# An MLP's down projection on one Trainium2 core: sums of weight blocks in a buffer of their own, conversions by the pair, and a fourth sweep

## The chip, the core and the metric

The kernel runs on one core of a Trainium2 chip. Its engines run side by side, each through its own list of instructions in order, and wait for each other by semaphores: TensorE (PE in the profile; PEld is its weight load), VectorE (DVE), ScalarE (ACT), GpSimd (POOL, unused here) and SyncE (SP, whose queue issues the loads). The metric is the device time of one execution in microseconds (us). Before the change its median over three runs is 2785.03 us (2783.8 to 2786.33).

## The reference

A decoder trunk with two layers, 256 tokens, a width of 2048 and float32 throughout:

```
h = h + retention(rms_norm(h))                 # layer 0
h = h + mlp(rms_norm(h)); h = h + gated_embedding(h, p)
k, v = rms_norm(h) @ w_kv
h = h + block_sparse_attention(rms_norm(h), k, v)   # layer 1
h = h + mlp(rms_norm(h)); h = h + gated_embedding(h, p)
return rms_norm(h)

def mlp(x): return square(relu(x @ w_up)) @ w_down   # w_up 2048 x 8192, w_down 8192 x 2048
```

The change concerns `... @ w_down`, once in each layer.

## The kernel before, in words

**Weights.** All weights come in pairs of units: one load of 1 MB fills a buffer `raw` (128 partitions, 2 units of 1024 columns). TensorE multiplies a rounded float32 format (`F32R`), so each operand is split into a rounded part `h` and a remainder `l`. `split` does it: a ScalarE cast writes `wh` (L237), then a VectorE subtraction writes `wl` (L238). A float32 product is three matmuls: xh by wh, xh by wl, xl by wh.

**The order.** The program is a list of units. `run` walks it: at unit i it issues the load for three pairs further, the conversions up to unit i + 4 (`LOOK`), the matmuls of unit i, and then small tasks that were set for that place with `at`: evacuations of PSUM, sums, norms. Each engine meets its instructions in the order in which this walk writes them. `raw` has three buffers, `wh` and `wl` five each. All weight loads go through SP's queue.

**The MLP.** The 8192 hidden columns are done in two halves. For each half, `phase_a` computes 32 tiles of 128 hidden columns by 256 tokens (64 units; the stage is called up), and `evac_up` squares and splits them into tiles `a`. Then the half's 4096 rows of `w_down` are swept: 16 pairs of 128-row blocks a and b, for 1024 output columns at a time (g = 0 and 1), so four stages (dn) in each layer.

**A sweep.** In a pair the work is a 2 by 2 block product: token halves (t = 0, 1) by the rows a, b, and rows a, b by two column halves of 512. Done plainly it is 8 block products, 24 matmuls of 512 columns, accumulated in four PSUM banks C00 to C11 (token half, column half). For six of the 16 pairs (`FAST`) it is 7 block products, 21 matmuls (the scheme of Strassen and Winograd): sums S1 to S4 of activation blocks (`combine`, made during up) meet sums of weight blocks, and three products (P1 and two more) and P5 go to banks of their own. The weight sums are made on VectorE inside `raw`, in place, just before their conversion: `mixed` (L583, L584) and `crossed` (L589, L590), two 128x512 subtractions each, and then one conversion:

```
def mixed(self, raw):
    v, r = self.nc.vector, raw[:, 0]
    v.tensor_sub(r[:, :512], r[:, 512:], r[:, :512])
    v.tensor_sub(r[:, 512:], raw[:, 1, :512], r[:, 512:])
    return self.halves(r)
```

A fast pair has four units (6, 3, 6 and 6 matmuls), a plain pair two of 12. Three of the four stages of a layer are such sweeps; the fourth (half 1, g = 1) is plain, by `phase_b`, one group of 512 columns after the other.

**The end of a sweep.** `done` adds the four C banks to the residual h (L651) after the last unit, and the P banks in the two units after it. In half 1, `finish` follows for each 512-column piece of h: squares with a sum on ScalarE (L258), eight transposes on TensorE into two `aux` banks (L271), and four tiles `x` for the next product, each a ScalarE scaling (L249) and a VectorE operation on the same PSUM bank (L250).

## Time and profile before

| what | us |
|---|---|
| median of three runs | 2785.03 |
| the profiled execution | 2782.08 |
| its span, first to last instruction | 2780.3 |
| PE, DVE, ACT busy in the span | 2736.0, 1949.6, 1365.0 |
| down projection, layer 0: half 0 (two sweeps), half 1 g = 0, half 1 g = 1 | 182.4, 89.3, 90.8 |
| down projection, layer 1: the same | 183.0, 89.1, 89.8 |

The stages of the last two rows run from 924.3, 1286.4, 1375.7, 2130.2, 2491.4 and 2580.5 us of the span. TensorE's granted clock is 0.997 over the span. Matmuls overlap: one of 512 columns is shown for 0.39 us, and the next starts 0.23 us after it, so the time that TensorE loses is read from the starts of matmuls and from its waits, not from its busy share.

### The profile page before, as it was taken

The page shows a single profiled execution, that of the slowest core. Times are in us where ns is not written, and L with a number is a line of the kernel's source. Part 1 is how long each engine was busy: PE and PEld are TensorE (multiplying, and loading weights), DVE is VectorE, ACT ScalarE, POOL GpSimd, SP SyncE. Part 2 cuts the span into 40 slices and gives each one's busy share as a digit, 9 for nine tenths or more (in the row PEclk, how much of TensorE's full clock was granted, in tenths as well). Part 3 has the DMA queues.
Part 4 walks back from the last instruction along what each step waited for, and adds up shares of the span by engine and source line. Part 5 has one row for each costly group of instructions (what it writes and reads, how often), then busy time and mean ns, then how long its engine had stood idle before and what let it go on. Part 6 is the DMA issues. An engine that isn't in the chain of part 4 may idle for free.

```text
span 2780.3 us, 35119 instructions
## 1 busy us (share of the span) xinstructions
PE 2736.0 (98%) x13644; PEld 2316.2 (83%) x13644; DVE 1949.6 (70%) x2833; ACT 1365.0 (49%) x1948; POOL 0.2 (0%) x4
## 2 busy tenths in 40 slices
PE   9999999999999999999999999999999999999998
PEld 8888888888888877888788888888888778887886
DVE  7766666654577777777756777775777778777655
ACT  6444444444444444444445555554444444444554
POOL 0000000000000000000000000000000000000000
PEclk9999999999999999999999999999999999999999
DMA  7455555555555445554465555445455545554553
GB/s 290 175 185 185 185 185 185 185 186 192 183 180 197 177 172 212 180 192 183 188 212 182 190 187 176 175 174 190 174 189 182 206 158 202 193 180 182 209 203 136
DMA packets 79458, 522.55 MB, mean 188 GB/s; under 512 B 8987, under 2 KB 12988, under 8 KB 17596
## 3 DMA queue, kind: packets, MB, share of 16 engines
q1 hardware_dynamic: 78476, 519.20, 52.0%
q8 instruction: 107, 1.75, 0.2%
q10 hardware_dynamic: 816, 1.11, 0.2%
q14 instruction: 59, 0.48, 0.0%
HBM read 517.39 MB, written 2.88 MB: 187 GB/s over the span
## 4 chain that ended last, share of the span: by engine, by line
PE 77%; DVE 13%; ACT 5%; DMA 3%; issue 2%; ACTq 0%; SPq 0%
PE up L171 12%; DVE wl L238 8%; PE up L169 6%; ACT wh L237 5%; PE qk L171 4%; PE aq L171 2%; PE ak L171 2%; DMA raw<-mlp_dn 2%; PE qk L169 2%; PE aq L169 1%; PE ak L169 1%; PE pu L714 1%; DVE raw L590 1%; DVE raw L584 1%; PE xt L271 1%
## 5 line engine op out<-in xcount | busy, mean ns | idle before, releaser
L238 DVE TENSOR_TENSOR wl<-raw,wh 128x1024 fp32r<-128x1024 f32 (+1 forms) x1043 | 1233.3, 1201 | 542.2 <-ACT wh L237 536.4
L237 ACT CAST wh<-raw 128x1024 fp32r<-128x1024 f32 (+1 forms) x1043 | 1055.7, 1031 | 648.7 <-DVE raw L584 102.9
L171 PE MATMUL up<-x,wh 128*128 128x512 f32 x2048 | 491.1, 391 | 4.2 <-DVE h L651 4.2
L171 PEld LDWEIGHTS up<-x,wh 128*128 128x128 f32 x2048 | 376.0, 188 | 77.3 <-ACT q L656 5.0
L169 PEld LDWEIGHTS up<-x,wl 128*128 128x128 f32 x2048 | 264.5, 192 | 10.4
L169 PE MATMUL up<-x,wl 128*128 128x256 f32 x2048 | 267.9, 283 | 0.0
L237 ACT CAST a<-s 128x256 fp32r<-128x256 f32 x128 | 52.0, 407 | 268.5 <-DVE s L638 268.5
L171 PE MATMUL qk<-x,wh 128*128 128x512 f32 x448 | 109.9, 392 | 0.0
L238 DVE TENSOR_TENSOR a<-s,a 128x256 fp32r<-128x256 f32 x128 | 54.5, 426 | 60.5 <-ACT a L237 60.5
L171 PEld LDWEIGHTS qk<-x,wh 128*128 128x128 f32 x448 | 81.8, 188 | 15.5
L249 ACT ACTIVATE x<-xt,g 128x256 fp32r<-128x256 f32 x112 | 52.4, 477 | 53.4 <-DVE x L250 40.6
L250 DVE SCALAR_TENSOR_TENSOR x<-xt,g,x 128x256 fp32r<-128x256 f32 x112 | 52.9, 481 | 27.3 <-ACT x L249 27.0
L242 ACT COPY t<-up 128x256 f32<-128x256 f32 x128 | 46.8, 366 | 41.1 <-PE up L171 40.6
L171 PE MATMUL aq<-x,wh 128*128 128x512 f32 x256 | 63.2, 391 | 0.0
L171 PE MATMUL ak<-x,wh 128*128 128x512 f32 x256 | 62.9, 391 | 0.0
L243 DVE TENSOR_TENSOR t<-t,up 128x256 f32<-128x256 f32 x128 | 53.2, 415 | 10.0 <-ACT t L242 10.0
L169 PEld LDWEIGHTS qk<-x,wl 128*128 128x128 f32 x448 | 57.4, 191 | 2.2
L169 PE MATMUL qk<-x,wl 128*128 128x256 f32 x448 | 58.1, 283 | 0.0
L634 DVE SCALAR_TENSOR_TENSOR s<-t 128x256 f32<-128x256 f32 x128 | 54.4, 425 | 4.4
L171 PEld LDWEIGHTS ak<-x,wh 128*128 128x128 f32 x256 | 46.7, 188 | 8.7
L171 PEld LDWEIGHTS aq<-x,wh 128*128 128x128 f32 x256 | 46.5, 188 | 8.7
L638 DVE TENSOR_TENSOR s<-s,rb 128x256 f32<-128x256 f32 x128 | 53.5, 418 | 0.0
(1122 smaller groups left out, 5171.8 us busy)
## 6 DMA issues: line engine op xcount, KB each, us to landing
raw<-mlp_up SPq DMA_DIRECT2D x128, 1024.0 KB, 4.8
raw<-mlp_dn SPq DMA_DIRECT2D x128, 1024.0 KB, 4.9
raw<-ret_in SPq DMA_DIRECT2D x94, 1024.0 KB, 4.8
raw<-att SPq DMA_DIRECT2D x48, 1024.0 KB, 4.8
raw<-ret_out SPq DMA_DIRECT2D x32, 1024.0 KB, 4.8
raw<-ple_gate SPq DMA_DIRECT2D x32, 1024.0 KB, 4.8
raw<-att_o SPq DMA_DIRECT2D x16, 1024.0 KB, 4.8
raw<-ple_up SPq DMA_DIRECT2D x4, 1024.0 KB, 4.9
```

Source lines behind the costliest of these rows:

```text
L169: mm(ps[:, S:], wl[:, c], rhs[k][:, :S], start=False, stop=end)
L171: mm(ps, wh[:, c], rhs[k], start=first and k == 0, stop=end)
L237: self.nc.scalar.copy(dst_h, src)
L238: self.nc.vector.tensor_sub(dst_l, src, dst_h.bitcast(F32))
L242: self.nc.scalar.copy(dst, ps[:, :S])
L243: self.nc.vector.tensor_add(dst, dst, ps[:, S:])
L249: self.nc.scalar.activation(t[:, :S], src, AF.Copy, scale=gs)
L250: self.nc.vector.scalar_tensor_tensor(t[:, S:], src, gs, t[:, :S].bitcast(F32), op0=ALU.mult, op1=ALU.subtract)
L271: self.nc.tensor.transpose(ps[:, o * P:(o + 1) * P], self.h[c][:, t, f * P:(f + 1) * P], self.ident)
L584: v.tensor_sub(r[:, 512:], raw[:, 1, :512], r[:, 512:])
L634: v.scalar_tensor_tensor(s, t, 0.0, t, op0=ALU.max, op1=ALU.mult)
L638: v.tensor_mul(s, s, st["rb"])
```

## The change

All four stages of a layer's down projection are sweeps of 16 pairs with six fast pairs each, now 2, 4, 6, 9, 11 and 13. Conversions are no longer one for each unit of 1024 columns: in a sweep a plain pair is converted by one cast and one subtraction of 2048 columns (`whole`), a fast pair by one of 1536 columns (`corner`: the three blocks that are used as they are) and one of 2048 columns (`wide`: the four sums). The sums are written into a buffer of their own, `tsum` (one buffer), by one VectorE addition of 2x512 columns and two of 512 (`sums`, L605 to L607 of the changed kernel), so that `raw` is free once it has been read. The operands `wh` and `wl` become rings of three buffers of a pair's width. A conversion is issued one buffer ahead: that of a pair when the buffer before it begins. A fast pair takes two buffers, one with 9 matmuls and one with 12. Loads are issued as soon as the pair three before has been converted.

At a sweep's end, the C banks of token half 0 are added to h after the first unit of pair 15, those of token half 1 after the second, and the P and Q banks in four steps during pairs 14 and 15, since no fast pair comes after 13. `finish` follows straight away, for two pieces of h at the end of each sweep of half 1.

In `evac_up`, relu(t) times the row scale is squared by a ScalarE activation (128 of them); a VectorE multiplication per tile goes. Of a fast pair's a-row tile only the used half is kept. The pool of activation buffers shrinks from 62 to 59, `cs` and `dec` move into it, and the bias rows of the attention are computed during the first up stage instead of 30 units before the end of the down projection.

VectorE, around a fast pair of a sweep. Before (one fast pair in the middle of the first sweep; `raw164` is its buffer, the rows around it are those of plain pairs):

```order
L238 TENSOR_TENSOR wl_7905<-raw163_7813,wh_7904 128x1024
L238 TENSOR_TENSOR wl_7913<-raw164_7854,wh_7912 128x1024
L238 TENSOR_TENSOR wl_7925<-raw164_7854,wh_7924 128x512
L583 TENSOR_TENSOR raw164_7854<-raw164_7854 128x512
L584 TENSOR_TENSOR raw164_7854<-raw164_7854 128x512
L238 TENSOR_TENSOR wl_7940<-raw164_7854,wh_7939 128x1024
L589 TENSOR_TENSOR raw164_7854<-raw164_7854 128x512
L590 TENSOR_TENSOR raw164_7854<-raw164_7854 128x512
L238 TENSOR_TENSOR wl_7958<-raw164_7854,wh_7957 128x1024
```

After (a fast pair, `raw_7523`, between the plain pairs of `raw_7479` and `raw_7548`):

```order
L250 TENSOR_TENSOR wl_7588<-raw_7479,wh_7587 128x2048
L605 TENSOR_TENSOR tsum_7605<-raw_7523 128x2x512
L606 TENSOR_TENSOR tsum_7605<-tsum_7605,raw_7523 128x512
L607 TENSOR_TENSOR tsum_7605<-tsum_7605,raw_7523 128x512
L250 TENSOR_TENSOR wl_7610<-raw_7523,wh_7609 128x1536
L250 TENSOR_TENSOR wl_7640<-tsum_7605,wh_7639 128x2048
L250 TENSOR_TENSOR wl_7653<-raw_7548,wh_7652 128x2048
```

The sums now stand ahead of both conversions of their pair, and no sum stands between two conversions.

ScalarE of the changed kernel, in layer 0, from the end of the sweep half 1, g = 0 into the next one (`sq` and `x` are tiles of `finish`, for the 512-column pieces of h named `h_89` and `h_90`; the three casts belong to the next sweep's pair 1 and to the two buffers of its first fast pair, pair 2):

```order
L270 ACTIVATE sq,ssq<-h_90 128x512 x2
L249 CAST wh<-raw 128x2048
L261 ACTIVATE x_0_10672<-xt,g 128x256
L261 ACTIVATE x_1_10675<-xt,g 128x256
L261 ACTIVATE x_2_10692<-xt,g 128x256
L261 ACTIVATE x_3_10695<-xt,g 128x256
L249 CAST wh<-raw 128x1536
L261 ACTIVATE x_4_10730<-xt,g 128x256
L261 ACTIVATE x_5_10733<-xt,g 128x256
L261 ACTIVATE x_6_10748<-xt,g 128x256
L261 ACTIVATE x_7_10751<-xt,g 128x256
L249 CAST wh<-tsum 128x2048
```

Two `sq` for `h_89` stand just ahead of the first row. VectorE stands likewise: the subtraction for pair 1, four `x`, the sums of pair 2, the subtraction for its first buffer, four `x`, the subtraction for its second. Before, `finish` fell at this place into a plain stage with conversions of 1024 columns; now it falls between the conversions of a sweep's first three pairs.

The diff, cut to what the text speaks of:

```diff
-FAST = [q in (2, 4, 7, 9, 12, 14) for q in range(16)]
+FAST = (2, 4, 6, 9, 11, 13)
+RAWS = 3
+RING = 3
...
+    def begin(self, src, pair):
+        s = {"first": len(self.units), "pair": len(self.pairs)}
+        self.pairs.append({"src": src, "pair": pair})
+        self.slots.append(s)
+        return s
...
     def unit(self, src, j, mm):
-        return self.part(src, j // 2, lambda raw: self.halves(raw[:, j % 2]), mm)
...
+        i = len(self.units)
+        if j % 2 == 0:
+            self.begin(src, j // 2)
+        s = self.slots[-1]
+        if i > 1:
+            self.prep.append((i - (SOON if i < 12 + SOON else LOOK), lambda: self.narrow(s, j % 2)))
+        self.units.append(lambda: mm(s["h"][:, j % 2], s["l"][:, j % 2]))
+        return i
...
+    def load(self, p):
+        t = p["raw"] = self.wp.tile([P, 2, UC], F32, name="raw", tag="raw", bufs=RAWS)
+        self.nc.sync.dma_start(t, self.io[p["src"]][p["pair"]])
+
+    def loads(self):
+        while self.loaded < min(len(self.pairs), self.spent + RAWS):
+            self.load(self.pairs[self.loaded])
+            self.loaded += 1
+
+    def operand(self, s):
+        for n in "hl":
+            s[n] = self.wp.tile([P, 2, UC], F32R, name=f"w{n}", tag=f"w{n}", bufs=RING)
+
+    def narrow(self, s, u):
+        raw = self.pairs[s["pair"]]["raw"]
+        if u == 0:
+            self.operand(s)
+        self.split(s["h"][:, u], s["l"][:, u], raw[:, u])
+        self.spent += u
+
+    def wide(self, s, src, n):
+        self.operand(s)
+        h, l = (s[x].rearrange("p a b -> p (a b)")[:, :n] for x in "hl")
+        self.split(h, l, src.rearrange("p a b -> p (a b)")[:, :n])
...
-        done = 2
-        for i in range(len(self.units)):
-            self.load(self.units[i][0] + 3)
-            while done <= i + (SOON if i < 12 else LOOK):
-                self.conv(done)
-                done += 1
-            wh, wl = self.ready.pop(i)
-            self.units[i][2](wh, wl)
+        self.prep.reverse()
+        for i, mm in enumerate(self.units):
+            self.loads()
+            while self.prep and self.prep[-1][0] <= i:
+                self.prep.pop()[1]()
+                self.loads()
+            mm()
...
-                st["dec"] = self.cp.tile([P, 384], F32, name=f"dec{hd}", tag="dec", bufs=2)
+                st["dec"] = self.slot("dec", (P, 384))
...
-    def sweep(self, name, src, first, fast, x, done):
...
-        for q, quick in enumerate(fast):
-            a, b = 2 * q, 2 * q + 1
-            if quick:
-                plan += [(q, self.low, [("C01", (q, "S4"), 0), ("C00", (b, 0), 1)]),
-                         (q, self.corner, [("P1", (a, 0), 0)]),
-                         (q, self.mixed, [("P5", (q, "S1"), 0), ("P7", (q, "S3"), 1)]),
-                         (q, self.crossed, [("P6", (q, "S2"), 0), ("C10", (b, 1), 1)])]
-            else:
-                plan += [(q, lambda raw: self.halves(raw[:, 0]), plain(a, False)),
-                         (q, lambda raw: self.halves(raw[:, 1]), plain(b, True))]
...
+    def sweep(self, name, src, first, pairs, x, done, rest):
+
+        banks, left = {}, {}
+        tags = {"P1": "y", "P5": "y", "Q6": "aux", "Q7": "aux"}
+
...
+            def mm():
+                h, l = (s[n].rearrange("p a (b c) -> p (a b) c", b=2) for n in "hl")
                 m = self.nc.tensor.matmul
...
+                for bank, which, j in ops:
+                    start = bank not in banks
...
+                    ps, (xh, xl) = banks[bank], x(*which)
+                    m(ps, xh, h[:, j], start=start, stop=False)
+                    m(ps, xh, l[:, j], start=False, stop=False)
+                    m(ps, xl, h[:, j], start=False, stop=left[bank] == 0)
...
+        for q in range(pairs):
+            a, b, due = 2 * q, 2 * q + 1, self.slots[-1]["first"]
+            s = self.begin(src, first + q)
+            if q in FAST:
+                last = q
+                add(s, [("C01", (q, "S4"), 1), ("C00", (b, 0), 2), ("P1", (a, 0), 0)])
+                t = {"first": len(self.units), "pair": s["pair"]}
+                self.slots.append(t)
+                e = add(t, [("P5", (q, "S1"), 0), ("Q6", (q, "S2"), 1), ("C10", (b, 1), 2), ("Q7", (q, "S3"), 3)])
+                self.prep.append((due, lambda s=s, t=t: self.sums(s, t)))
+                self.prep.append((due, lambda s=s: self.corner(s)))
+                self.prep.append((s["first"], lambda t=t: self.wide(t, t["t"], 2 * UC)))
+            else:
+                for r in range(2):
+                    i = add(s, [(f"C{r}{c}", (k, r), j) for c, ks in ((0, ((a, 0), (b, 2))), (1, ((a, 3), (b, 1)))) for k, j in ks])
+                self.prep.append((due, lambda s=s: self.whole(s)))
+        for n, fn in enumerate(rest(banks)):
+            self.at(e + 1 + n, fn)
+        self.at(i - 1, lambda: done(banks, 0, i))
+        self.at(i, lambda: done(banks, 1, i))
...
+    def whole(self, s):
+        self.wide(s, self.pairs[s["pair"]]["raw"], 2 * UC)
+        self.spent += 1
+
+    def corner(self, s):
+        self.wide(s, self.pairs[s["pair"]]["raw"], 3 * UC // 2)
+        self.spent += 1
+
+    def sums(self, s, t):
+        v = self.nc.vector
+        t["t"] = self.wp.tile([P, 2, UC], F32, name="tsum", tag="tsum")
+        r, o = (z.rearrange("p a (b c) -> p (a b) c", b=2) for z in (self.pairs[s["pair"]]["raw"], t["t"]))
+        v.tensor_add(o[:, 0::3], r[:, 0:2], r[:, 3:4].to_broadcast([P, 2, 512]))
+        v.tensor_add(o[:, 1], o[:, 0], r[:, 1])
+        v.tensor_add(o[:, 2], o[:, 1], r[:, 2])
...
-                act[n] = self.slot(f"a{n}", dt=F32R)
...
-                v.tensor_mul(s, s, st["rb"])
-                self.split(act[n][:, :S], act[n][:, S:], s)
...
+                v.scalar_tensor_tensor(t, t, 0.0, st["rb"], op0=ALU.max, op1=ALU.mult)
+                nc.scalar.activation(t, t, AF.Square)
+                if q in FAST and n % 2 == 0:
+                    j = FAST.index(q)
+                    if j % 2 == 0:
+                        st["c"] = self.slot("ac", (P, 4, P), F32R)
+                    act[n] = st["c"][:, 2 * (j % 2):2 * (j % 2) + 2]
+                    self.split(act[n][:, 0], act[n][:, 1], t[:, :P])
+                else:
+                    act[n] = self.slot(f"a{n}", dt=F32R)
+                    self.split(act[n][:, :S], act[n][:, S:], t)
+                if n % 2:
+                    if q not in FAST:
+                        pair.pop(q)
+                        return
+                    yield
+                    combine(q)
...
+            def done(banks, t, i, g, half=half):
+                for c in range(2):
+                    h = self.h[2 * g + c][:, t]
+                    v.tensor_add(h, h, banks[f"C{t}{c}"])
+                if half and t:
+                    for c in range(2):
+                        self.finish(2 * g + c, i + 2 * c, gains)
...
+                def one():
+                    z["q"], z["u"] = self.slot("q"), self.slot("u")
+                    nc.scalar.copy(z["q"], banks["P1"])
+                    v.tensor_add(h(0, 0), h(0, 0), z["q"])
+
+                def two():
+                    v.tensor_sub(z["q"], z["q"], banks["Q6"])
+                    v.tensor_add(z["u"], z["q"], banks["P5"])
+                    v.tensor_sub(h(0, 1), h(0, 1), z["u"])
+
+                def three():
+                    v.tensor_add(z["q"], z["q"], banks["Q7"])
+                    v.tensor_add(h(1, 0), h(1, 0), z["q"])
+
+                def four():
+                    v.tensor_add(z["q"], z["q"], banks["P5"])
+                    v.tensor_sub(h(1, 1), h(1, 1), z["q"])
+                return [one, two, three, four]
...
             for g in range(2):
-                if half and g:
-                    for c in (2, 3):
-                        e = len(self.units) + n - 1
-                        self.phase_b(f"dn{c}_", src, (4 + c) * n, n, lambda k: act[k], lambda banks, c=c, e=e: evac_dn(c, banks, e))
-                else:
-                    self.sweep(f"dn{half}{g}_", src, (half * 2 + g) * n, FAST, x, lambda banks, i, g=g, done=done: done(banks, i, g))
+                self.sweep(f"dn{half}{g}_", src, (half * 2 + g) * n, n, x, lambda banks, t, i, g=g, done=done: done(banks, t, i, g),
+                           lambda banks, g=g, rest=rest: rest(banks, g))
...
-            st["x"], self.xx = self.xx, {}
-        self.at(b + 2, hold)
+            self.xx = {}
+        self.at(b + 2, lambda: st.update(x=self.xx))
+        self.at(b + 11, hold)
...
-            tc.tile_pool(name="slots", bufs=62) as sp, \
+            tc.tile_pool(name="slots", bufs=59) as sp, \
...
+        c.bias_rows(len(c.units) + 10)
         c.mlp(0, [G_PLE0])
-        c.bias_rows(len(c.units) - 30)
...
-        parts = [cut_s(dn[:FH, :1024]), cut_s(dn[:FH, 1024:]), cut_s(dn[FH:, :1024]), cut_b(dn[FH:, 1024:])]
+        parts = [cut_s(dn[:FH, :1024]), cut_s(dn[:FH, 1024:]), cut_s(dn[FH:, :1024]), cut_s(dn[FH:, 1024:])]
```

More of the change, by code (lines that the diff above doesn't have):

```diff
@@ L97, in at @@
     def at(self, i, fn):
         self.tasks.setdefault(i, []).append(fn)
-    def load(self, q):
-        if q >= len(self.pairs) or q in self.raws:
-            return
-        src, pair = self.pairs[q]
-        t = self.raws[q] = self.wp.tile([P, 2, UC], F32, name=f"raw{q}", tag="raw", bufs=3)
-        self.nc.sync.dma_start(t, self.io[src][pair])
-    def operand(self, cols=UC):
-        return [self.wp.tile([P, cols], F32R, name=f"w{n}", tag=f"w{n}", bufs=LOOK + 1) for n in "hl"]
-    def halves(self, raw):
-        wh, wl = self.operand(raw.shape[-1])
-        self.split(wh, wl, raw)
-        return wh, wl
@@ L157, in small @@
     def small(self, name):
-        return self.wp.tile([P, S], F32, name=name, tag="small", bufs=8)
+        return self.wp.tile([P, S], F32, name=name, tag="small", bufs=4)
     def mm_a(self, ps, wh, wl, rhs, first, last, turned=False):
@@ L342, in start @@
         load_x(3)
-        self.raws[1] = raw2 = self.wp.tile([P, 2, UC], F32, name="raw2", tag="raw", bufs=3)
+        raw2 = self.pairs[1]["raw"] = self.wp.tile([P, 2, UC], F32, name="raw2", tag="raw", bufs=RAWS)
         for v in range(2):
@@ L347, in start @@
         load_x(5)
-        self.load(2)
+        self.load(self.pairs[2])
+        self.loaded, self.spent = 3, 1
         load_x(6)
@@ L566, in mm @@
                     if start:
                         banks[bank] = self.bank(f"{name}{bank}_", *((tags[bank], 2) if bank in tags else ()))
-                    ps, (xh, xl), c = banks[bank], x(*which), cut[j]
-                    m(ps, xh, wh[:, c], start=start, stop=False)
-                    m(ps, xh, wl[:, c], start=False, stop=False)
-                    m(ps, xl, wh[:, c], start=False, stop=stop)
-            i = self.part(src, first + q, conv, mm)
-        self.at(i, lambda: done(banks, i))
@@ L575, in low @@
[L575 to L591 removed]
+                    left[bank] -= 1
@@ L674, in evac_dn @@
-            def evac_dn(c, banks, i):
-                for t in range(2):
-                    h = self.h[c][:, t]
-                    v.tensor_add(h, h, banks[t])
-                self.finish(c, i, gains)
+                v.scalar_tensor_tensor(t, t, 0.0, st["rb"], op0=ALU.max, op1=ALU.mult)
[9 more added lines that the diff above has]
+                    self.split(act[n][:, :S], act[n][:, S:], t)
```

147 lines of the change are left out of this document (43 added, 104 removed).

## The prediction

> **What bounds the kernel now.** First the page's busy shares and its chain of what ended last.
>
> ```profile
> PE 2736.0 (98%) x13644; PEld 2316.2 (83%) x13644; DVE 1949.6 (70%) x2833; ACT 1365.0 (49%) x1948; POOL 0.2 (0%) x4
> PE 77%; DVE 13%; ACT 5%; DMA 3%; issue 2%; ACTq 0%; SPq 0%
> ```
>
> TensorE is the bound, but a fifth of the chain runs through VectorE, ScalarE and loads. Where is read from the busy times by stage (from:to, length, then PE, PEld, DVE, ACT, POOL, granted clock). Rows: up of layer 0, dn half 0, up half 1, dn half 1 g = 0, g = 1; then dn of layer 1.
>
> ```profile
> 744.80:924.30 179.50, 179.50 (x1037) 158.76 (x1036) 135.72 (x237) 88.06 (x139) 0.00 (x0) 1.00 0.53 187
> 924.30:1106.70 182.40, 171.69 (x734) 137.64 (x732) 141.29 (x158) 85.63 (x95) 0.00 (x0) 0.99 0.49 186
> 1106.70:1286.40 179.70, 179.70 (x1024) 158.89 (x1025) 138.67 (x227) 85.22 (x129) 0.00 (x0) 0.99 0.53 188
> 1286.40:1375.70 89.30, 84.70 (x368) 68.28 (x366) 68.31 (x77) 44.28 (x50) 0.00 (x0) 1.00 0.49 187
> 1375.70:1466.50 90.80, 90.80 (x411) 74.65 (x412) 53.60 (x61) 41.34 (x56) 0.00 (x0) 1.00 0.60 199
> 2130.20:2313.20 183.00, 171.48 (x733) 137.70 (x733) 141.47 (x158) 85.97 (x95) 0.00 (x0) 0.99 0.49 185
> 2313.20:2491.40 178.20, 178.19 (x1024) 157.52 (x1025) 138.65 (x227) 85.21 (x129) 0.00 (x0) 1.00 0.54 190
> 2491.40:2580.50 89.10, 84.61 (x368) 68.28 (x367) 68.35 (x77) 44.27 (x50) 0.00 (x0) 1.00 0.50 188
> 2580.50:2670.30 89.80, 89.80 (x408) 74.59 (x409) 53.04 (x59) 41.35 (x56) 0.00 (x0) 1.00 0.54 191
> ```
>
> Up and the plain stages keep TensorE full; the sweeps do not. What a matmul costs when nothing holds it: fifteen of 512 columns between these two starts of the plain stage (timeline), 3.40/15 = 0.2267 us each.
>
> ```profile
> 1386.18 0.39 PE L211 MATMUL dn__11392<-wh,a 128*128 128x512 f32 x1
> 1389.58 0.39 PE L211 MATMUL dn__11393<-wh,a 128*128 128x512 f32 x1
> ```
>
> A sweep has 10 x 24 + 6 x 21 = 366 matmuls, 83.0 us. Six sweeps take 182.4 + 89.3 + 183.0 + 89.1 = 543.8 us, 45.8 above 6 x 83.0. The list of waits says at what (engine, line, waited for: total, times, longest):
>
> ```profile
> PE up L171 <- DVE h L651: 4.2, 2, 2.1
> PE dn_P__18937 L570 <- DVE wl L238: 3.0, 4, 0.8
> PE dn_C__7831 L569 <- DVE t L243: 2.1, 1, 2.1
> ACT wh L237 <- DVE raw L584: 102.9, 31, 6.6
> ACT wh L237 <- DVE raw L590: 94.4, 35, 2.7
> ```
>
> At each sweep's end TensorE waits for the C banks (L651), at its start for a PSUM bank of up (L243), and inside it for conversions late behind the in-place sums. One such place, with its clock rows below:
>
> ```profile
> 1002.92 0.69 DVE L590 TENSOR_TENSOR raw<-raw 128x512 f32<-128x512 f32 x1
> 1003.73 3.89 ACT L237 CAST wh<-raw 128x1024 fp32r<-128x1024 f32 x4 [2.70 <-DVE raw L590]
> 1004.81 2.36 DVE L238 TENSOR_TENSOR wl<-raw,wh 128x1024 fp32r<-128x1024 f32 x2 [1.19 <-ACT wh L237]
> 1006.09 0.50 PE L570 MATMUL dn_P__7928<-wl,sh 128*128 128x512 f32 x1 [0.77 <-DVE wl L238]
> 1013.00:1015.00 2.00, 0.00 (x0) 0.00 (x0) 2.00 (x4) 1.53 (x2) 0.00 (x0) 1.00 1.04 438
> 1016.00:1019.40 3.40, 3.40 (x9) 2.63 (x9) 3.33 (x6) 0.00 (x0) 0.00 (x0) 0.50 0.66 277
> ```
>
> The sum L590, then the cast, then the subtraction, then the matmul: a serial chain. The last two rows: after about 2 us without a matmul TensorE is granted half its clock for 3.4 us, which costs 1.7 us more. (At 1373 us the same wait was followed by clock 1.00, so it does not come every time.)
>
> **The change part by part.** Fewer matmuls: the two plain stages become sweeps, 12 fast pairs more, 3 matmuls less each: 36 x 0.2267 = **8.2 us**, on the path.
>
> The floor: eight sweeps without a wait take 8 x 83.0 = 664.0 us. The eight stages take 543.8 + 90.8 + 89.8 = 724.4; in them lie also the transposes of three pieces of h in each layer (below: from 1383.92 to 1384.71, 0.8 each, 4.8 in all) and the bias matmul with its wait (90.8 - 89.8 = 1.0), both paid in the new kernel too. Up half 1 of layer 0 is 1.5 longer than that of layer 1, in the slow clock's tail.
>
> ```profile
> 1383.92 1.03 PE L271 MATMUL xt<-ident,h 128*128 128x128 f32 x8
> ...
> 1384.71 0.48 PE L211 MATMUL dn__11392<-wh,a 128*128 128x512 f32 x1
> ```
>
> So at most 724.4 + 1.5 - 664.0 - 5.8 = **56.1 us** can go: 8.2 of matmuls, 48 of waits. Which waits stay? For that the new conversions need a price; the groups by form have the widths that exist:
>
> ```profile
> L238 DVE TENSOR_TENSOR wl<-raw,wh 128x1024 fp32r<-128x1024 f32 x1002 | 1208.3, 1223 | 541.3 <-ACT wh L237 536.0 <-PE up L171 3.7 <-PE aq L171 0.5
> L238 DVE TENSOR_TENSOR wl<-raw,wh 128x512 fp32r<-128x512 f32 x39 | 26.6, 686 | 0.9 <-ACT wh L237 0.4
> L237 ACT CAST wh<-raw 128x1024 fp32r<-128x1024 f32 x1002 | 1033.9, 1049 | 641.7 <-DVE raw L584 102.9 <-DVE raw L590 94.4 <-DMA raw<-mlp_dn 36.6
> L237 ACT CAST wh<-raw 128x512 fp32r<-128x512 f32 x39 | 23.9, 616 | 6.9 <-PE dn_C__8444 L571 4.8 <-PE dn_C__18832 L571 2.1
> L399 DVE TENSOR_TENSOR qc<-qr,cs x8: 681/684/685, 54.3 to 511.9; 128x512 f32<-128x512 f32 x8
> L258 ACT ACTIVATE sq<-h 128x512 f32<-128x512 f32 x48 | 29.9, 625 | 36.1 <-DVE h L523 15.1 <-DVE h L677 7.6 <-DVE h L727 6.8
> L250 DVE SCALAR_TENSOR_TENSOR x<-xt,g,x 128x256 fp32r<-128x256 f32 x112 | 52.9, 481 | 27.3 <-ACT x L249 27.0
> L249 ACT ACTIVATE x<-xt,g 128x256 fp32r<-128x256 f32 x112 | 52.4, 477 | 53.4 <-DVE x L250 40.6 <-PE xt L271 10.4 <-DMA g<-gains 2.0
> ```
>
> 2048 columns: by the slope, VectorE 1223 + 2 x 537 = 2.30 us, ScalarE 1049 + 2 x 433 = 1.92; at most two of 1024, 2.45 and 2.10. I take the slope, since 512 and 1024 show a fixed part. 1536 columns: 1.76 and 1.48. The sums: 1.22 + 0.69 + 0.69, with two gaps 2.68; L399 reads through a broadcast and is no dearer than a plain 512.
>
> In a sweep the pair after a fast one is tightest. Its ring buffer is that of the pair ahead of the fast one. From TensorE's last start there + 0.23: 0.16 until that matmul's end, 0.12 to ScalarE (1003.61 to 1003.73 above), cast 1.92, 0.03, subtraction 2.30, 0.06 to TensorE: 4.59. Due: 21 matmuls and one more (the first needs only `wh`), 4.99. **Margin 0.40; with the dear ends 0.07.** The fast pair's second buffer: sums from 4.5 to 7.2, subtraction 1536 to 8.9, cast 7.3 to 9.2, subtraction to 11.6; due 10.2 + 2.04 + 0.23 = 12.5. VectorE's work in a fast and a plain pair is 2.30 + 2.68 + 1.76 + 2.30 = 9.0 of 45 x 0.2267 = 10.2. So the middle of a sweep should have no wait; below nothing it cannot go, TensorE being full.
>
> Loads: each now waits at the head of SP's queue for the subtraction of the pair three before; the further weight loads stand behind it, and a few small ones that are read units later. A buffer of `raw` is free some 8.9 us into a cycle at the latest, and the next load into it is first read more than 10 us later, against a landing of 4.9:
>
> ```profile
> raw<-mlp_dn SPq DMA_DIRECT2D x128, 1024.0 KB, 4.9
> ```
>
> Sweep ends: C banks of token half 0 are evacuated beside 12 matmuls (2.7 us for two additions of 0.69): the 2 us wait of L651 goes. Sweep starts out of up: the last two up tiles' evacuations stand between the first conversions, at some 0.4 us an operation. From the end of tile 30's matmuls: copy 0.5, cast of pair 0 2.4, subtraction 4.7 (due 5.8); then the operations on tile 30 and the copy of tile 31 to 6.25 on ScalarE, cast of pair 1 8.1, subtraction 10.4 (due 11.3); tile 31 to 12.1 on VectorE, sums 14.8, first subtraction of pair 2 16.5 (due 16.7), cast 16.8, second subtraction 19.15, due 18.75: wait 0.4, at four places **1.6**. The 2 us wait of L243 goes.
>
> What comes late instead: half 1, g = 0 into g = 1, where `finish` meets a sweep's start. Clock zero is the end of pair 15. TensorE's own times without a wait: pair 0 with eight transposes to 6.25, pair 1 with eight to 12.5, pair 2's first buffer to 14.55 (9 matmuls). ScalarE and VectorE, each in its written order: the last C addition ends at 1.0; of the squares (0.62 each, L258) three can only follow the last additions, to 2.2; the cast of pair 1 stands behind them, to 4.1; its subtraction 6.4, due 6.5. Then four `x`: on each of the two PSUM banks ScalarE's second operation waits for VectorE's first (L249 and L250 name each other as releasers), so they alternate at some 0.5 us: VectorE's last ends at 9.35. Sums to 12.0, first subtraction of pair 2 to 13.75, due 12.7: **wait 1.1**, and the first buffer ends at 15.65. Four more `x` follow, ScalarE's last at 16.2, and behind it stands the cast of the sums, 18.1; subtraction 20.4, due 15.65 + 0.23: **wait 4.6**. Late next would be pair 3's subtraction, 22.7, but it is due only at 23.2. So 5.7 per layer, and in holes of over 2 us, so with the half clock as above, 1.7. In half 1, g = 1 the four `x` of two pieces stand among the copies of the embedding's first units: about **1.0** per layer. Left in all: 1.6 + 2 x (5.7 + 1.7 + 1.0) = **18.4**.
>
> [...]
>
> At nothing: 128 squares on ScalarE and 128 multiplications fewer on VectorE lie in up, where TensorE is busy all 179.5 and ScalarE 88; without cover the squares would cost 128 x 0.4 (the cast of the same width):
>
> ```profile
> L237 ACT CAST a<-s 128x256 fp32r<-128x256 f32 x128 | 52.0, 407 | 268.5 <-DVE s L638 268.5
> ```
>
> The bias rows pay at another place. The pool's three buffers less: tiles in its place wait, if at all, for matmuls long past. Elsewhere the conversions keep their four units.
>
> Sum: 2782.1 - 56.1 + 18.4 = 2744.4 for the profiled execution; the median lies 2.95 above it: **2747 us**.
>
> **The rivals.** (A) The finish is hidden after all: VectorE and ScalarE have run ahead further than I reckon, no wait there. For it: the middle leaves ScalarE half idle. Against: the chain begins at pair 15's last matmul. All 56.1 go, less some 3: 2732.
> (B) The wide conversion comes too late. A pair's first 1024 columns are usable only when all 2048 are done; with margins of 0.07 to 0.40 a price 0.4 above my dear end costs 48 places (six in each of eight sweeps) x 0.33 to 0.4, 16 to 19 us: 2765. For it: nothing is shown at that width; against: both bounds fit.
> [...]
> (C) The change doesn't do what it says: the chain of sum, cast and subtraction is as long from `tsum`, and only matmuls go: 2785 - 8 = 2777.
> (D) Slower: VectorE becomes the bound of the sweeps, if a sum with strided output and broadcast input runs at half rate. Then 9.0 + 2.7 = 11.7 per fast and plain pair against 10.2, 48 x 1.5 = 72 us more than the floor: 2785 - 56 + 72 = 2801. It decides above 11.4. Against it: L399.
>
> **How the numbers follow.** Forecast 0.66 (2738 to 2758), A 0.14, B 0.13, C 0.04, D 0.03. The range leaves out C, D and A's and B's far ends: 2730 to 2768. What a measurement can tell from no change is about 0.2%, 5.6 us: faster 0.95, same 0.02, slower 0.03.
>
> **What would show it.** Sweeps of half 0 together at 166 to 168 us against 182.4; `wl` of 2048 columns at 2.3 us; no wait of TensorE for L672's additions of a C bank; in half 1, g = 1 two holes of TensorE at pair 2, one for the first subtraction and one for the cast and subtraction of `tsum`, then the clock at 0.5. Wrong would be: a wait of the same size at each plain pair behind a fast one (B), VectorE full through a sweep (D), or up stages longer than 179.7.

## The result, and the profile after

The changed kernel takes 2753.4 us (median of four runs, 2751.07 to 2754.37) against 2785.68 for the kernel before on the same chip: a ratio of 0.9883, 95% interval 0.9866 to 0.99. Forecast were 2747, with 2730 to 2768 as the range. The profiled execution took 2752.92 us, its span 2750.5; the two spans differ by 29.8. One of the four executions of e5 below took 3372.51 us at a granted clock of 0.752, and e5's ratio is that of the other three.

The page after: busy shares, and the chain of what ended last.

```profile
PE 2722.4 (99%) x13608; PEld 2310.3 (84%) x13608; DVE 1924.7 (70%) x2543; ACT 1406.5 (51%) x1926; POOL 0.2 (0%) x4
PE 81%; DVE 10%; ACT 7%; issue 2%; DMA 0%; ACTq 0%; SPq 0%; DVEq 0%
```

36 matmuls are gone (13644 before), and loads are gone from the chain (3% before). VectorE and ScalarE still hold 17% of it (18% before). The busy times by stage say where (from:to, length, PE, PEld, DVE, ACT, POOL, granted clock). Layer 0: half 0, half 1 g = 0, g = 1, the embedding; then the same of layer 1.

```profile
925.80:1093.60 167.80, 167.07 (x734) 137.12 (x733) 139.38 (x109) 83.75 (x54) 0.00 (x0) 1.00 0.57 207
1271.70:1355.07 83.37, 83.24 (x368) 68.61 (x366) 69.48 (x55) 42.00 (x29) 0.00 (x0) 1.00 0.60 213
1355.07:1446.70 91.63, 87.36 (x383) 71.19 (x382) 72.90 (x61) 47.79 (x42) 0.00 (x0) 0.98 0.52 188
1446.70:1464.00 17.30, 14.81 (x66) 11.79 (x66) 11.56 (x16) 11.93 (x25) 0.00 (x0) 0.90 0.34 122
2116.00:2284.00 168.00, 167.05 (x734) 137.12 (x733) 139.85 (x109) 83.75 (x54) 0.00 (x0) 1.00 0.58 207
2462.10:2545.50 83.40, 83.28 (x368) 68.64 (x367) 69.51 (x55) 42.00 (x29) 0.00 (x0) 1.00 0.60 213
2545.50:2637.30 91.80, 87.53 (x384) 71.28 (x383) 73.35 (x62) 48.09 (x43) 0.00 (x0) 0.98 0.52 187
2637.30:2652.40 15.10, 12.84 (x66) 10.62 (x65) 9.77 (x14) 10.79 (x22) 0.00 (x0) 1.00 0.41 140
```

The embedding stages of the kernel before, up to the gate's first matmul, in the same view:

```profile
1466.50:1478.30 11.80, 11.80 (x58) 9.85 (x57) 6.98 (x10) 10.22 (x19) 0.00 (x0) 1.00 0.49 179
2670.30:2682.10 11.80, 11.80 (x57) 9.85 (x57) 6.97 (x10) 10.16 (x19) 0.00 (x0) 1.00 0.53 184
```

| stage, layer 0 / layer 1 | before | after |
|---|---|---|
| half 0, two sweeps | 182.4 / 183.0 | 167.8 / 168.0 |
| half 1, g = 0 | 89.3 / 89.1 | 83.4 / 83.4 |
| half 1, g = 1 (plain before) | 90.8 / 89.8 | 91.6 / 91.8 |
| embedding | 11.8 / 11.8 | 17.3 / 15.1 |

The three quarters that were sweeps already gain 41.2 us. The fourth, which the change made a sweep, has 18 matmuls and eight transposes less in each layer and is longer all the same. The embedding behind it loses 8.8, of which 1.8 are those transposes, which now stand there: in e10 below the embedding has the same matmuls and no wait, and takes 12.7 in each layer. What TensorE waits for (total, times, longest):

```profile
PE xt L283 <- DVE x L262: 4.5, 2, 2.3
PE dn_P__10774 L567 <- ACT wh L249: 2.0, 1, 2.0
PE dn_P__20461 L567 <- ACT wh L249: 2.0, 1, 2.0
PE dn_P__10774 L568 <- DVE wl L250: 1.8, 1, 1.8
PE dn_P__20461 L568 <- DVE wl L250: 1.8, 1, 1.8
```

Past the program's start, every wait of more than 0.5 us is at one of two places: the P5 bank's first matmuls in half 1, g = 1 (at pair 2), and the transposes `xt` in the embedding. Inside the sweeps, from pair 3 to pair 15, no matmul starts more than 0.24 us after the one before, but for one at 0.32 where a half clock ends (2569.89). Below, a wait is counted so, as time between two starts beyond the usual; it is a little more than the idle time in the rows (2.16 and 2.10 us at layer 0's pair 2, for 2.0 and 1.8).

The conversions, from the groups by form:

```profile
L250 DVE TENSOR_TENSOR wl<-raw,wh 128x2048 fp32r<-128x2048 f32 x80 | 181.9, 2290 | 81.9 <-ACT wh L249 81.8
L249 ACT CAST wh<-raw 128x2048 fp32r<-128x2048 f32 x80 | 153.1, 1913 | 90.5 <-PE dn_C__7464 L569 12.6 <-PE dn_C__17151 L569 12.6 <-PE dn_C__17684 L569 12.1
L250 DVE TENSOR_TENSOR wl<-raw,wh 128x1536 fp32r<-128x1536 f32 x48 | 84.0, 1751 | 0.0
L605 DVE TENSOR_TENSOR tsum<-raw 128x1024 f32<-128x1024 f32 x48 | 58.5, 1218 | 0.0
```

### The profile page after: what moved, and what is told of

The parts are those of the page before. It is cut to its first block, busy times and chain, and to the rows that moved or that the text cites. A ratio compares the mean times of both kernels' runs of the same rounds, so it can differ in the third digit from the quotient of the medians.

```text
span 2750.5 us, 33950 instructions
## 1 busy us (share of the span) xinstructions
PE 2722.4 (99%) x13608; PEld 2310.3 (84%) x13608; DVE 1924.7 (70%) x2543; ACT 1406.5 (51%) x1926; POOL 0.2 (0%) x4
## 3 DMA queue, kind: packets, MB, share of 16 engines
q8 instruction: 107, 1.75, 0.3%
## 4 chain that ended last, share of the span: by engine, by line
PE 81%; DVE 10%; ACT 7%; issue 2%; DMA 0%; ACTq 0%; SPq 0%; DVEq 0%
PE up L183 9%; DVE wl L250 6%; PE up L181 5%; ACT wh L249 4%; PE qk L183 4%; PE aq L183 2%; PE ak L183 2%; PE qk L181 2%; PE aq L181 1%; PE ak L181 1%; ACT t L651 1%; DVE t L650 1%; ACT a L249 1%; DVE t L255 1%; PE y L492 1%
## 5 line engine op out<-in xcount | busy, mean ns | idle before, releaser
L250 DVE TENSOR_TENSOR wl<-raw,wh 128x1024 fp32r<-128x1024 f32 (+3 forms) x843 | 1121.5, 1350 | 396.3 <-ACT wh L249 396.0
L249 ACT CAST wh<-raw 128x1024 fp32r<-128x1024 f32 (+3 forms) x843 | 952.3, 1151 | 370.3 <-issue 77.9
L249 ACT CAST wh<-tsum 128x2048 fp32r<-128x2048 f32 x48 | 91.8, 1913 | 161.0 <-DVE tsum L607 129.0
L651 ACT ACTIVATE t<-t 128x256 f32<-128x256 f32 x128 | 53.5, 418 | 228.5 <-DVE t L650 228.5
L250 DVE TENSOR_TENSOR wl<-tsum,wh 128x2048 fp32r<-128x2048 f32 x48 | 110.0, 2292 | 29.1 <-ACT wh L249 29.1
L250 DVE TENSOR_TENSOR a<-t,a 128x256 fp32r<-128x256 f32 x104 | 44.3, 426 | 95.9 <-ACT a L249 95.9
L270 ACT ACTIVATE sq<-h 128x512 f32<-128x512 f32 x48 | 30.1, 627 | 62.0 <-DVE h L534 27.7
L605 DVE TENSOR_TENSOR tsum<-raw 128x1024 f32<-128x1024 f32 x48 | 58.5, 1218 | 0.0
```

What stands on the lines that cost most here:

```text
L249: self.nc.scalar.copy(dst_h, src)
L250: self.nc.vector.tensor_sub(dst_l, src, dst_h.bitcast(F32))
L270: self.nc.scalar.activation(self.slot("sq"), self.h[c][:, t], AF.Square, accum_out=self.ssq[:, t, c:c + 1])
L605: v.tensor_add(o[:, 0::3], r[:, 0:2], r[:, 3:4].to_broadcast([P, 2, 512]))
L651: nc.scalar.activation(t, t, AF.Square)
```

## The experiments

All are edits of the changed kernel; none leaves out any of its computation, and e7, e8, e9 and e12 add work. Each was timed beside the kernel before, whose median was 2785.5 to 2786.3.

| edit | us | ratio to before, 95% |
|---|---|---|
| the change itself | 2753.4 | 0.9866 to 0.99 |
| e1: first fast pair 3 | 2741.25 | 0.9828 to 0.9857 |
| e2: last finish spaced | 2748.27 | 0.9853 to 0.9882 |
| e3: e1 and e2 | 2736.76 | 0.9811 to 0.9841 |
| e4: conversions in pieces | 2737.67 | 0.9811 to 0.9844 |
| e5: e1, e2 and e4 | 2728.74 | 0.9781 to 0.9813 |
| e6: sums in place | 2802.03 | 1.0045 to 1.0075 |
| e7: 1.05 us more on ScalarE per plain pair | 2802.04 | 1.0045 to 1.0075 |
| e8: 2.1 us more on VectorE per fast pair | 2803.25 | 1.0048 to 1.0082 |
| e9: matmuls that only fill the holes | 2747.77 | 0.985 to 0.9879 |
| e10: fourth quarter plain | 2742.35 | 0.983 to 0.9859 |
| e11: e5 with the fourth quarter plain | 2734.95 | 0.9804 to 0.9833 |
| e12: 0.72 us more on VectorE per fast pair | 2756.76 | 0.9878 to 0.9911 |

### e1: one more plain pair ahead of the first fast one

```diff
-FAST = (2, 4, 6, 9, 11, 13)
+FAST = (3, 5, 7, 9, 11, 13)
```

> The fast pairs are moved from 2, 4, 6, 9, 11, 13 to 3, 5, 7, 9, 11, 13: one plain pair more ahead of the first, nothing else. Theory (order): at a sweep's start the last evacuations and the finish stand ahead of the first conversions on ScalarE and VectorE, and a plain pair gives VectorE back 3.1 us (24 matmuls, 5.4 us, against 2.3 of subtraction). Of the 25.2 us of waits of the changed kernel the ones at pair 2 out of up go (1.0 and 0.4 per layer), and of the 5.2 us into half 1, g = 1 some 2 stay, in waits too short for the half clock (1.65 less): 6.3 us less per layer, 2741 us. Rival 1 (the chain of sums, cast and subtraction is late at whichever pair is the first fast one): the same waits one pair later, 2753. Rival 2 (all of it was slack that one pair gives back): no wait left at any sweep start, 2736. Rival 3 (six fast pairs with only one plain between each have no slack to recover in): waits of 0.1 to 0.7 in the middle of the sweeps, 2760.

2741.25 us. Its longest waits of TensorE in the sweeps:

```profile
PE dn_C__10655 L568 <- DVE wl L250: 1.4, 1, 1.4
PE dn_C__20342 L568 <- DVE wl L250: 1.3, 1, 1.3
```

At the first fast pair into half 1, g = 1 the waits are 2.2 us per layer (1.6 and 0.6) instead of 5.0, and the half clock behind them is gone; out of up nothing is left at the fast pair, only 0.6 and 0.8 at pair 0. No wait in the middle although now only one plain pair stands between any two fast ones. The order theory holds in place and size.

### e2 and e3: the last finish spaced

```diff
-                    self.finish(2 * g + c, i + 2 * c, gains)
+                    self.finish(2 * g + c, i + (4 if g else 2) * c, gains)
```

> Only the last quarter's finish is moved: its second piece of h is transposed four units after the first, not two, so among the gate's units instead of the embedding's. Theory: the holes of 2.45 and 2.42 us at the transposes in the embedding stage are waits for the two PSUM banks, whose four x stand on ScalarE among casts of 1.04 and copies of 0.58 in units of only 12 matmuls; they go, and so does the half clock behind one of them (1.7): 6.5 us less, 2747. Rival (ScalarE is simply full in those four units): the wait moves on to the embedding's or the gate's first matmuls, 2752 or 2753.

2748.27 us. No transpose waits any more (the 4.5 us of L283 are gone); two waits of 0.5 stay in each embedding stage, of its matmuls and the gate's first for ScalarE's copies. So the rival is right for 1 us per layer of what was won.

> Both of the edits above. Theory: they act at different places and add up: 2741 and 2747 against 2753.4 give 2734.7. Rival: they do not add up, since what is freed at one place is lost at the next: 2741.

2736.76, where the two edits' own gains add to 2736.1: they act apart.

### e4: the wide conversions in pieces

```diff
-        self.split(h, l, src.rearrange("p a b -> p (a b)")[:, :n])
+        src = src.rearrange("p a b -> p (a b)")
+        for c in range(0, n, UC):
+            d = slice(c, min(c + UC, n))
+            self.split(h[:, d], l[:, d], src[:, d])
```

> Each wide conversion is cut: 2048 columns into 1024 and 1024, 1536 into 1024 and 512, cast and subtraction of the first piece before those of the second. Theory: in the middle of a sweep TensorE waits for nothing, so nothing can be won there; at the starts the first piece is ready 1.9 us earlier after a cast (1.05 + 1.22 against 1.91 + 2.29), so the 2.10 us hole, the 0.5 to 0.6 at pair 2 and the 0.5 to 0.7 at pair 0 go and the half clock perhaps with them: some 4 us less per layer, 2745, with no wait in the middle. Rival 1 (the fixed cost of 0.15 us for each further piece on VectorE and 0.19 on ScalarE eats the margin of 0.4): waits in the middle, 2760. Rival 2 (the starts are set by the work that stands ahead, not by the width): 2753.

2737.67, 7 us better than expected. What TensorE waits for (the rows left out are the same two in layer 1 and the program's start):

```profile
PE xt L286 <- DVE x L265: 4.5, 2, 2.2
PE dn_P__10916 L570 <- ACT wh L252: 1.0, 1, 1.0
...
PE dn_P__10916 L571 <- DVE wl L253: 0.8, 1, 0.8
```

The waits out of up (4.1) are gone; into half 1, g = 1 the 0.23, 0.72, 2.16 and 2.10 us became 1.15 and 1.14, and two of three half clocks did not come. The middle was full before and is full now, so the price of the additional instructions (176 more on each engine) shows nowhere. Neither hole is gone, as I had expected of the second, but both shrank by 1.0; the first, which I had expected to stay, ends with the cast of the sums, and its first 1024 columns are ready 0.86 us sooner.

### e5: all three

> First fast pair 3, the last quarter's finish spaced by four units, and each wide conversion cut into pieces of at most 1024 columns. Theory (what is left at the sweep starts with the first two edits, 6.1 us in all, are waits for a whole subtraction; the pieces take them, and the middle has 1.16 us of VectorE to give per fast and plain pair, of which the pieces cost 0.46): 2736.8 less 6 is 2731, with no wait inside a sweep. Rival (the pieces and the later first pair take the same waits, and the dearer conversions now bind, since only one plain pair stands between any two fast ones): 2737 or more, with waits inside the sweeps.

2728.74 us: 57 us below the kernel before and 25 below the change as made, 2 better than expected. The whole list of its waits:

```profile
PE warm L398 <- DVE zero L391: 1.5, 1, 1.5
PE qk L213 <- ACT wh L252: 0.8, 1, 0.8
PE pu L737 <- ACT pu L739: 0.4, 2, 0.2
PE gt__11533 L226 <- ACT pu L739: 0.3, 1, 0.3
PE gl__21396 L226 <- ACT pu L739: 0.3, 1, 0.3
```

The first two are the program's start. The profile lists no wait in any of the eight sweeps.

### e10 and e11: was the fourth sweep worth it?

The fourth quarter goes back to plain pairs, with the new conversions (in half 1 the a-row tiles are then kept whole):

```diff
-                           lambda banks, g=g, rest=rest: rest(banks, g))
+                           lambda banks, g=g, rest=rest: rest(banks, g), () if half and g else FAST)
```

> The fourth quarter (half 1, g = 1) in plain pairs only, with the wide conversions; the first three are sweeps with fast pairs as in the changed kernel. 36 matmuls more, 8.2 us. Theory (a fast pair that comes as early as pair 2 behind a finish costs more in waits than its three matmuls bring): of the 6.8 and 6.9 us of waits and half clock at this sweep's start only some 0.5 per layer stay, since a plain pair needs neither sums nor a second conversion: 2753.4 + 8.2 - 12.7 = 2749, so the fourth quarter's part of the change cost time as it was made. Rival (the finish is late for any pair): the waits stay and the matmuls come on top, 2761.

2742.35: with 36 matmuls more it is 11 us faster than the changed kernel, and 6.6 faster than expected. Its longest waits inside the program:

```profile
PE dn_C__10651 L568 <- DVE wl L250: 0.7, 1, 0.7
PE dn_C__20296 L568 <- DVE wl L250: 0.7, 1, 0.7
```

Into the fourth quarter 1.2 us per layer stay of 6.8 and 6.9 (with the half clock), and, what I had not seen, the embedding's 4.7 and 2.6 are gone too: a plain quarter has no P and Q banks to add at its end, and the last C bank is in h 0.9 us after the embedding's first matmul in e10 (1446.55) and 3.7 us after it in the changed kernel (1450.49), so the finish comes sooner. 8.2 - 11.3 - 7.3 is -10.4, against -11.1 measured.

> The same in the kernel with all three edits (first fast pair 3, spaced finish, conversions in pieces), which showed no wait at that place. Theory: only the matmuls are left, 2728.7 + 8.2 = 2736.9. Rival (the plain quarter is faster in itself, by its easier conversions): 2729 or less.

2734.95: 6.2 us slower than e5. The plain quarter also lacks e5's four waits of the embedding and the gate (2.1), so 36 matmuls cost 8.3. The sign of this part of the change hangs on its surroundings: it costs 11 us as made, and saves 6 once the starts are mended.

### e6: the sums in place

```diff
+                self.prep.append((due, lambda s=s: self.corner(s)))
                 self.prep.append((due, lambda s=s, t=t: self.sums(s, t)))
-                self.prep.append((due, lambda s=s: self.corner(s)))
-                self.prep.append((s["first"], lambda t=t: self.wide(t, t["t"], 2 * UC)))
+                self.prep.append((s["first"], lambda t=t: self.crossed(t)))
...
+    def crossed(self, t):
+        self.wide(t, t["t"], 2 * UC)
         self.spent += 1
...
-        t["t"] = self.wp.tile([P, 2, UC], F32, name="tsum", tag="tsum")
+        t["t"] = self.pairs[s["pair"]]["raw"]
```

> One part of the change undone: the sums are written over the raw tile, so they stand behind its 1536-column conversion and the raw buffer is held until the sums are converted; the widths stay. Theory (the buffer of their own lets the sums run ahead): VectorE's order becomes subtraction 1536 (1.75), sums (2.68), cast of the sums (1.91), subtraction (2.29), a serial chain from the end of the subtraction before: 979.03 in the changed kernel's sweep + 1.75 + 2.7 + 1.95 + 2.3 = 987.7 against a need at 987.02, so 0.7 to 0.8 at the second buffer of each of 48 fast pairs: 2753 + 36 = 2789, about the kernel before. Rival (the pair conversions alone brought the gain, the buffer only memory): 2753 to 2757.

2802.03 us, slower than the kernel before. A fast pair in the middle of the first sweep, in its timeline:

```profile
961.50 0.69 DVE L610 TENSOR_TENSOR raw<-raw 128x512 f32<-128x512 f32 x1
962.30 5.53 ACT L249 CAST wh<-raw 128x2048 fp32r<-128x2048 f32 x3 [5.21 <-DVE raw L610]
...
966.60 0.50 PE L568 MATMUL dn_P__7524<-wl,sh 128*128 128x512 f32 x1 [0.64 <-DVE wl L250]
```

The cast waits for the in-place sum (L610), the matmul for the subtraction: the serial chain of the kernel before is back. Its price lies elsewhere than I had put it: in the middle 26 waits of 0.7 to 1.0, 21.7 us in all (the first fast pair after two plain ones has none), and at the starts 13 us more, with half clocks behind most of them, 8.5 more; the remaining 5 lie mostly at the sweeps' ends and in the embedding. The edit also holds `raw` longer, and ScalarE now waits for loads of `w_down`, 12 times and 39.3 us in all (never in the changed kernel), but none of the 26 waits in the middle lies within 14 us behind one of these casts. The buffer of their own, with the earlier release of `raw` that goes with it, is worth 48.6 us, more than the whole change.

### e7, e8 and e12: the two margins

```diff
+        self.nc.scalar.copy(h[:, :1024], z[:, :1024])     # e7, in whole, ahead of the split
...
+        v.tensor_add(o[:, 2], o[:, 1], r[:, 2])           # e12: once more; e8: this twice and o[:, 1] once
```

> In the sweeps the plain pairs' first 1024 columns are cast twice: 1.05 us more between the release of the ring buffer and the subtraction. Theory (margin at the plain pair after a fast one 0.44 in the trace, 0.40 in the prediction): 0.6 at each of 48 places, 29 us, and up to 1 at the sweep starts that already wait, 2753 + 29 + 6 = 2788. Rival (ScalarE is half idle and takes it as slack): 2753 to 2758.

2802.04. A plain pair behind a fast one in e7's timeline:

```profile
962.00 1.06 ACT L598 CAST wh<-raw 128x1024 fp32r<-128x1024 f32 x1 [1.06 <-PE dn_C__7466 L569]
965.02 2.29 DVE L250 TENSOR_TENSOR wl<-raw,wh 128x2048 fp32r<-128x2048 f32 x1 [1.77 <-ACT wh L249]
967.37 0.50 PE L568 MATMUL dn_C__7440<-wl,a 128*128 128x512 f32 x1 [0.47 <-DVE wl L250]
```

The matmul would have started at 966.74 and starts at 967.37: 0.63 late for 1.08 us more, so the margin was 0.45. The next one follows after 0.34 us, not 0.23, so the place costs 0.74: 40 places, 29.8 us. The other eight are the sweeps' first, where 12 us come on top, and half clock lasts 6.8 us longer in all, 3.4 lost. So the middle cost what was expected, and the starts more than twice the 6.

> Three more additions of 512 columns per fast pair (a repeat of the last two sums), 2.1 us of VectorE. Theory (VectorE has 1.16 us to give per fast and plain pair: 9.0 of 10.2): 11.2 of work per 10.2, so about 1.0 at each of 48 fast pairs, and some at the starts: 2753 + 48 + 6 = 2807. Rival (VectorE is busy only 70% of the span, and runs ahead over the stretches with two or three plain pairs): a third of that or less, under 2770.

2803.25. 28 of the 40 later fast pairs wait, about 1.2 us each, 32.4 in all, and 17 us come at the starts and by half clocks. The twelve that do not are pair 9 of each sweep, which has two plain pairs ahead of it, as the rival had it, and in four sweeps pair 4, behind a long wait at pair 2.

> One more addition of 512 columns per fast pair in the changed kernel, 0.72 us of VectorE: 9.75 of 10.2 us per fast and plain pair. Theory (1.16 us to give, of which three additions took more than all): no wait in the middle, and up to 0.7 more at each of the eight sweep starts, which wait already: 2753 to 2759. Rival (every us more on VectorE costs its share, as three additions cost 50 us in all): 2753 + 50/3 = 2770.

2756.76. From 960 to 1000 us, e8 and then e12:

```profile
960.00:1000.00 40.00, 38.65 (x167) 30.70 (x166) 36.05 (x31) 17.86 (x11) 0.00 (x0) 1.00 0.53 189
```

```profile
960.00:1000.00 40.00, 40.00 (x179) 33.10 (x178) 34.32 (x25) 21.76 (x13) 0.00 (x0) 1.00 0.57 209
```

With 0.72 us more VectorE is busy for 34.3 of 40 us and TensorE for all of them, with 178 weight loads; with 2.1 more it gets through 166. In e12 the middle has no wait, and six of the eight starts wait some 0.7 longer, as expected. The price of work on VectorE is no line here but a corner, which lies between 0.72 and 2.1 us more per fast and plain pair; by the sum of durations it is 1.2.

### e9: filling the holes

Ahead of both waits of the P5 bank in half 1, g = 1, eight matmuls whose result is overwritten or never read; in the embedding's hole sixteen transposes of the same kind:

```diff
+                    if start and bank == "P5" and name == "dn11_":
+                        for _ in range(8):
+                            m(ps, *old, start=True, stop=True)
```

> Matmuls that compute nothing are put where TensorE waits in the changed kernel: eight of 512 columns (1.8 us) ahead of each of the two holes at pair 2 of half 1, g = 1 (2.16 and 2.10 us), and sixteen transposes of 128 columns (1.7 us) into the hole of 2.4 us in the embedding stage. They add 32 + 32 instructions that fit inside the holes, so no wait gets longer. Theory (in the traces so far every half clock begins on a grid of 3.413 us that is fixed within a run, and follows a piece of the grid in which TensorE stood idle for more than about half; 1.77 and less were not followed, 1.87 and more were, but for one of 1.89 and one of 1.79): with 0.3 to 0.7 us idle left the three half clocks go, 1.6 + 1.7 + 1.7, and the time falls from 2753.4 to 2748.4 though TensorE does more. Rival 1 (the half clock has nothing to do with the holes, or goes by the wait's kind): 2753. Rival 2 (the added matmuls run past the holes): 2755 or more.

2747.77 us: 64 instructions more and 5.6 us less, though the P5 bank's two matmuls start as late as in the changed kernel (2.40 and 2.33 us after the computation's own matmul ahead of them, against 2.39 and 2.33). What the windows show is told in the last section.

## Why the prediction was right, and where not

**Right: the middle of the sweeps.** The prices held: 2.29, 1.91, 1.75 and 2.67 us for the sums against 2.30, 1.92, 1.76 and 2.68. The margin of 0.40 is 0.45 in e7, and VectorE's slack of 1.2 us bears 0.72 more (e12) and not 2.1 (e8). So no wait from pair 3 on, and rivals B, C and D fall (A falls by the holes below): B's place, the plain pair behind a fast one, has none of its 48 waits. No matmul of up or of the next sweep waits for the C banks' additions (L672) any more, and the half-0 sweeps are 167.8 and 168.0, as forecast (166 to 168). One sign of being wrong did come: up of half 0 in layer 0 takes 180.5 us, over the 179.7 named. The 1.0 over the 179.5 before is the bias rows' two matmuls, which now stand there; the other three up stages take 178.1, 179.5 and 178.1, so the squares cost nothing there.

That a pair's first 1024 columns are usable only when all 2048 are done I weighed for B's place alone, where pieces change nothing (e4 has no wait there either). I should have held it against my own list of remaining waits: there e4 shows pieces to be worth 15.7 us (2737.67 against 2753.4).

**Right in mechanism, 0.5 per layer too dear: the finish into half 1, g = 1.** Forecast were 5.7 and the half clock of 1.7; measured are 5.2 in each layer (0.23 at pair 1; 0.72, 2.16 and 2.10 at pair 2) and 1.6 and 1.7. The pair and both of its buffers are the ones named; e1 shows that the order ahead of them sets the wait, e4 that the width does as well.

**Wrong in size: the starts out of up, "at four places 1.6".** Measured are 1.55, 0.40, 1.77 and 0.40, 4.1 in all: the forecast 0.4 out of half 1's up, four times that out of half 0's. The step that failed, at half 0 alone, is "From the end of tile 30's matmuls: copy 0.5, cast of pair 0 2.4, subtraction 4.7 (due 5.8)". ScalarE at that place (tile 31 ends at 925.8 and takes 5.6, so tile 30's matmuls end at 920.2), and in the last row its copy of tile 30 in half 1, where those end at 1266.1:

```profile
921.12 0.42 ACT L651 ACTIVATE t<-t 128x256 f32<-128x256 f32 x1 [1.82 <-DVE t L650]
921.57 0.41 ACT L249 CAST a<-t 128x256 fp32r<-128x256 f32 x1
921.88 0.36 ACT L254 COPY t<-up 128x256 f32<-128x256 f32 x1
922.15 1.90 ACT L249 CAST wh<-raw 128x2048 fp32r<-128x2048 f32 x1
...
1266.32 0.37 ACT L254 COPY t<-up 128x256 f32<-128x256 f32 x1 [1.35 <-PE up L183]
```

In half 0 the square and the cast of the tile before stand ahead of the copy and wait for VectorE; the copy ends 2.0 us after the matmuls, not 0.5. I counted tile 30's operations and took tile 29's for done, and the whole chain slid by 1.5: pair 0 waits 0.5 to 0.7, and pair 2's buffers 0.44 and 0.59. In half 1 they are done, the copy waits for TensorE, and each step of the forecast holds to 0.2 us, up to the last subtraction (18.9 us after tile 30's matmuls, forecast 19.15). The difference is a backlog: in half 0's up the copies of tiles 5 to 29 start 2.2 to 6.4 us after their matmuls (in the kernel before 0.5 to 5.0), in half 1's 0.2 to 1.4. What builds it up after tile 4 no run here takes apart.

**Wrong in size: "about 1.0" per layer in the embedding.** Measured are 4.7 (1.7 of it a half clock that I had not forecast there) and 2.6. This was the one term with no working. ScalarE there, and TensorE's two groups of transposes:

```profile
1454.70 0.47 ACT L261 ACTIVATE x<-xt,g 128x256 fp32r<-128x256 f32 x1 [0.55 <-DVE x L262]
1455.07 1.04 ACT L249 CAST wh<-raw 128x1024 fp32r<-128x1024 f32 x1
1456.01 1.07 ACT L736 COPY pu<-pu 128x512 f32<-128x512 f32 x2
1456.96 0.50 ACT L261 ACTIVATE x<-xt,g 128x256 fp32r<-128x256 f32 x1
```

```profile
1456.27 0.60 PE L283 MATMUL xt<-ident,h 128*128 128x128 f32 x4
1459.15 0.63 PE L283 MATMUL xt<-ident,h 128*128 128x128 f32 x4 [2.29 <-DVE x L262]
```

Four `x` take 5.3 us (1453.67 to 1459.00): a cast and two copies stand between the second, here the first row, and the third, and the second and fourth wait for VectorE's. The second group of transposes needs the PSUM bank that the fourth frees. Written out like the other terms, this would have been seen; e2 takes it away.

**The sum.** Left in all were 25.1 us, not 18.4: 2.5 more at the starts, 5.3 more in the embedding, 1.1 less at the finish. That is 6.7 of the 8.5 us between the 2744.4 worked out and the 2752.9 profiled; the start of the program was 0.5 later, and 1.3 is spread too thin to name.

**Overlooked, though the numbers stood there.** The 8.2 us of matmuls were set against a floor over all eight stages. Set against the waits that I myself put behind the fourth sweep (5.7 + 1.7 + 1.0 per layer, 16.8) they say that this part of the change loses 8.6 us. Measured by e10: 11.

## What to carry to other kernels

Split a forecast by the parts that could be left out, and set each part's gain against the waits that it alone brings: here the part that saved matmuls cost time as it was made, and the others, which move conversions and additions, brought all of the gain (of these only the buffer of the sums was taken back by itself, in e6). Wide conversions were no better than pieces where TensorE never waits (e4 has no wait there either) and worse at a stage's first use (by 15.7 us in all, e4), so cut them there. At a seam between stages, write down every instruction of the two stages in the order of each engine, the tile before included, and give no term a price without that list.
